# Attention products with V issued two steps at a time, one step's exponentials in the gates' buffers, gates loaded in the last unit

## The chip, the cores and the metric
The kernel runs on one core of a Trainium2 chip. Its engines are TensorE (PE, with its weight loads as PEld), VectorE (DVE), ScalarE (ACT), GpSimd (POOL) and SyncE (SP), which here issues all DMAs, in order. The metric is the device time of one execution in microseconds; lower is better.

## What is computed
Two layers of a backbone that mixes three branches over 1024 latent and 256 context tokens, model width 1024. Each layer normalises and modulates its input, projects it once, and feeds (A) a chunked, bidirectional gated delta recurrence with four heads, (B) attention with four heads, in which latent tokens read latents and context and context tokens read context alone, and (C) a gated short convolution. The outputs are gated, concatenated, sent through one output projection and added to the stream, times a gate; after the last layer only the latents are kept, with a final norm. The core of the attention and of the recurrence in the reference:

```python
def block(q_blk):                                  # attention, per block of 128 queries
    s = jnp.einsum("bqhd,bkhd->bhqk", q_blk, k).astype(F32) * scale
    p = jax.nn.softmax(s, axis=-1).astype(v.dtype)
    return jnp.einsum("bhqk,bkhd->bqhd", p, v)

def step(s, xs):                                   # recurrence, per chunk of 64 tokens
    w_n, u_n, qk_n, qd_n, kd_n, gt_n = xs
    v_new = u_n - jnp.einsum("bhck,bhkv->bhcv", w_n, s)
    o_n = jnp.einsum("bhck,bhkv->bhcv", qd_n, s) + jnp.einsum("bhij,bhjv->bhiv", qk_n, v_new)
    s = s * gt_n[..., None, None] + jnp.einsum("bhck,bhcv->bhkv", kd_n, v_new)
    return s, o_n
...
x = x + gate_x * (mix_x @ w_out)                   # after each layer, and ctx with gate_c in the first
```

## The kernel before
Scores are kept transposed: keys lie on the partitions, queries along the row. The attention of a layer is cut into units of one pair of heads and one group of queries: 512 queries against ten tiles of 128 keys (four units in each layer), and in the first layer two units more of 256 context queries against the two context tiles. A unit of ten key tiles has five steps of two tiles.

A step goes as follows. `a_scores` (L1131) makes, for two key tiles and two heads, four score banks of three products each (a split of the operands in a high and a low part, `kh`, `kl`, or `kc` for the context keys; the products are recorded at line L84) and has ScalarE write their exponentials into two `probT` tiles (L1143). POOL adds the exponentials of all steps up in `vt` (L1129); of the last step, VectorE does one head's part, in a layer's last unit both (L1127). `a_pv` (L1148) issues four products with V (L1159). These are column-tiled: the two heads of the pair write partitions 0 to 63 and 64 to 127 of one bank `po` with a `tile_position` (0, 64r), while the score products fill the whole array. `a_out` (L1162) follows the last step of a unit: two column-tiled products with ones that sum `vt` over the keys (L1170), a reciprocal (L1173), two multiplications (L1174 and, on POOL, L1175) and the store of `bx_d`.

PE's order in this part is the order of the program, written out by hand: the PVs of a step stand behind the scores of the next one, so that ScalarE has a step's time for its exponentials. Between scores, `filler` issues the row maxima of the next unit (`a_max`, L1102, reduced by DVE at L1104), and `sch.tick` moves a planned clock on; lanes whose time has come then issue their next piece. The lanes are the two directions of the recurrence (P products L1226, `vd` and `ring` from DVE L1228 and POOL L1232; V products L1236, DVE L1240, ACT L1244; D products L1249, L1254, L1255; operands arrive in slots of `ring` over SP: vr_d, nn_d, kt_d, qk_d, row_d), the loads of the output weights (`load_wo`, L1311), and the first finish lanes of the output stage (loads of `ot`, `raw`, `za`, `xt`; L1344 to L1354; then the products of `mix` with w_out, recorded at L84). Outside this part a planner orders PE by modelled times, as it does for the other engines everywhere; so an edit can also move PE's rows far away from it.

Buffers are pools by tag: T5 holds five tiles of 128x1024 values, taken by `probT`; B4 two, taken by the context keys' tiles and then by the two gate vectors, `gate_x` and `gate_c` (each broadcast to 128 partitions, 512 KB; in the last layer the second is the final norm's weight); P2 seven, among them `zb` and `wr`. `load_wo` waits for the recurrence to have read its first state, loads both gates, and then 16 pieces `wr` of w_out, which ScalarE (L75, `wo_hi`) and POOL or DVE (L76, `wo_lo`) split. The gates are first used at L1368, in the output stage.

Of the kernel before, what the change touches and what calls it, by code (L numbers as in the profile page):

```python
# [13 lines left out]
D = 1024  # L14
# [8 lines left out]
GROUPS = ((0, 512), (512, 512), (1024, 256))  # L23
# [5 lines left out]
def kernel(  # L29
# [27 lines left out]
    def st(shape, tag, dtype=F32, name=None):  # L57
        return sb.tile(shape, dtype, tag=tag, name=name or tag, bufs=BUFS[tag])

    def const(shape, name, dtype=F32):  # L60
        return sb.tile(shape, dtype, tag=name, name=name, bufs=1)

    def bank():
        return ps.tile([128, 512], F32, tag="b", name="bank", bufs=8)

    def dram(shape, name):
        return dr.tile(shape, F32, tag=name, name=name, bufs=1)

    V, A, P, T, S = nc.vector, nc.scalar, nc.gpsimd, nc.tensor, nc.sync
# [11 lines left out]
    def mm3(outp, pairs):  # L81
        n = len(pairs)
        for q, (lh, rh) in enumerate(pairs):
            T.matmul(outp, lhsT=lh, rhs=rh, start=q == 0, stop=q == n - 1)  # L84
# [36 lines left out]
    sch = Sched()  # L121

    class Flags(dict):
# [3 lines left out]
        def ok(self, *keys):  # L127
# [41 lines left out]
    LY = [dict(A2=const([128, 2, KD], f"A2{l}"), B2=const([128, 2, KD], f"B2{l}"), col=const([128, 102], f"col{l}"),  # L169
               gate=dram([2, D], f"gate_d{l}")) for l in range(DEPTH)]  # L170
# [145 lines left out]
    for l in range(DEPTH):  # L316
        last = l == DEPTH - 1
# [115 lines left out]
        def parts(n_tok):  # L433
            return [(g, t0, n, 2 + t0 if g < 2 else 1030) for g, (t0, n) in enumerate(GROUPS) if t0 < n_tok]
# [485 lines left out]
        if l == 0:  # L920
# [16 lines left out]
            for t in (0, 1):  # L937
                for hf in range(2):
                    pms = [bank(), bank()]
                    for k4 in range(2):  # L940
                        for j in range(2):
                            q = 2 * hf + j
# [47 lines left out]
        for q, b in enumerate(z2):  # L990
            g = parts(n_tok_a)[-1][0]
# [90 lines left out]
        def a_keys(g):  # L1082
            return [8, 9] if g == 2 else list(range(NT))

        def key_tile(h, kt):
            if kt < NX:
                return kh[:, h, kt * 128:(kt + 1) * 128], kl[:, h, kt * 128:(kt + 1) * 128]
            return kc[:, 0, h, (kt - NX) * 128:(kt - NX + 1) * 128], kc[:, 1, h, (kt - NX) * 128:(kt - NX + 1) * 128]
# [21 lines left out]
        def a_shift(u):  # L1110
            m = GROUPS[u["g"]][1] // 128
            pn = bank()
            T.transpose(pn[0:2 * m, 0:128], u["nm"][:, 0:2 * m], ident)
            rw = st([8, 128], "h5", F32R, name="rw")
            copy_a(rw[0:2 * m], pn[0:2 * m, 0:128])
            for r, gh in enumerate(heads(u)):
                S.dma_start(out=Q[gh]["qt"][96:97, 0, 0:128 * m].bitcast(F32).rearrange("p (j t) -> p j t", j=m), in_=rw[r * m:(r + 1) * m].bitcast(F32))

        def a_sums(u, kts, pts, rs=(0, 1)):
            n = GROUPS[u["g"]][1]  # L1120
            keys = a_keys(u["g"])
            for r in rs:
                acc = vt[:, 5 + r, 0:n]
                ab_ = [pts[r][:, kk, 0:n] for kk in range(2)]
                for a0, a1 in [(ab_[0], ab_[1])] if kts[0] == keys[0] else [(acc, ab_[0]), (acc, ab_[1])]:
                    if kts[-1] == keys[-1] and (r == 0 or u is units[-1]):
                        V.tensor_tensor(out=acc, in0=a0, in1=a1, op=ALU.add)  # L1127
                    else:
                        P.tensor_tensor(acc, a0, a1, ALU.add)  # L1129

        def a_scores(u, kts, filler):  # L1131
            g, pair = u["g"], u["pair"]
            n = GROUPS[g][1]
            first = kts[0] == a_keys(g)[0]
            pts = [st([128, 2, 512], "T5", name="probT") for _ in range(2)]
            for kk, kt in enumerate(kts):
                for r in range(2):
                    h = 2 * pair + r
                    qt = Q[g, h]["qt"]
                    hi, lo = key_tile(h, kt)  # L1140
                    pb = bank()[:, 0:n]
                    mm3(pb, [(hi[0:97], qt[0:97, 0, 0:n]), (hi[0:96], qt[0:96, 1, 0:n]), (lo[0:96], qt[0:96, 0, 0:n])])
                    A.activation(out=pts[r][:, kk, 0:n], in_=pb, func=ACTF.Exp)  # L1143
                    if kk and not first:
                        a_sums(u, kts, pts, (r,))
                    sch.tick(0.0014 * n)
                    filler()
            return pts  # L1148

        def a_pv(u, kts, pts):  # L1150
            g, pair = u["g"], u["pair"]
            n = GROUPS[g][1]
            keys = a_keys(g)
            if "po" not in u:
                u["po"] = bank()
            for kk, kt in enumerate(kts):
                for r in range(2):
                    hh = 2 * pair + r
                    T.matmul(u["po"][64 * r:64 * r + 64, 0:n], lhsT=vx[:, kt, hh * 64:hh * 64 + 64], rhs=pts[r][:, kk, 0:n],  # L1159
                             start=kt == keys[0], stop=kt == keys[-1], tile_position=(0, 64 * r))  # L1160
# [121 lines left out]
        def heads(u):  # L1282
            return [(u["g"], 2 * u["pair"] + r) for r in range(2)]
# [21 lines left out]
        nu = len(units)  # L1305
        wo = []

        gates = []
        wof = Flags()

        def load_wo():  # L1311
            while not recurred.ok(0, 1):
                yield 1.0
            for nm, src in (("gate_x", LY[l]["gate"][0]), ("gate_c", final_norm_g if last else LY[l]["gate"][1])):
                gates.append(st([128, D], "B4", name=nm))
                S.dma_start(out=gates[-1], in_=src.partition_broadcast(128))
            for q in range(2):
                wh = st([128, KD, 512], "B16", F32R, name="wo_hi")
                wl = st([128, KD, 512], "B16", F32R, name="wo_lo")
                yield from load_wo_half(q, wh, wl)  # L1320
                wo.append((wh, wl))
            wof.put(0, 3.0)

        def load_wo_half(q, wh, wl):
            for k in range(KD):
                wr = st([128, 512], "P2", name="wr")
                S.dma_start(out=wr, in_=w_out[l, 128 * k:128 * k + 128, 512 * q:512 * q + 512])
                yield 1.5
                split(wr, wh[:, k], wl[:, k], P if k % 2 else V)
                yield 1.5  # L1330
# [70 lines left out]
            hdone.put(i, 1.0)  # L1401

        sch.add(load_wo())
        prev = ending = None
        aheads = []
        for x_, u in enumerate(units):
            keys = a_keys(u["g"])
            steps = [keys[q:q + 2] for q in range(0, len(keys), 2)]
            nxt = units[x_ + 1] if x_ + 1 < nu else None
            if nxt:  # L1410
                mg = a_max(nxt)

            def filler():
                if nxt and (len(steps) == 1 or 1 <= q <= 3):
                    for _ in range(6 if len(steps) == 1 else 2):
                        if next(mg, u) is not u:
                            sch.tick(0.25)

            for q, kts in enumerate(steps):
                if nxt and q == 0:  # L1420
                    sch.until(lambda: nxt["g"] in QA)
                    for gh in heads(nxt):
                        q_head(*gh)
                    sch.tick(2.4)
                    if nxt["pair"] == 1 and nxt["g"] + 1 in qgs:
                        sch.add(q_rows(nxt["g"] + 1))
                if nxt and q == 4:
                    a_shift(nxt)
                pts = a_scores(u, kts, filler)
                if prev:  # L1430
                    a_pv(*prev)
                    if prev[0] is not u:
                        next(ending)
                        for gh in heads(prev[0]):
                            Q.pop(gh)
                    sch.tick(0.0035 * GROUPS[prev[0]["g"]][1])
                if q == 0:
                    a_sums(u, kts, pts)
                if q == len(steps) - 1:
                    ending = a_out(u)  # L1440
                    next(ending)
                prev = (u, kts, pts)
                if nxt and len(steps) == 1:
                    for _ in mg:
                        pass
                    a_shift(nxt)
                if (x_, q) in (((nu - 1, 1), (nu - 1, 3)) if last else ((nu - 3, 3), (nu - 2, 0))):
                    sch.until(lambda: len(recurred) == 2)
                    ahead(len(aheads))
                    aheads.append(q)  # L1450
        a_pv(*prev)
        Q.clear()
        ahead(2)
        sch.tick(2.0)
# [94 lines left out]
```

## Time and profile before
| | us |
|---|---|
| median of three runs | 1718.66 (1716.41 to 1720.2) |
| the profiled execution, its own time | 1723.55 |
| its span on the core | 1721.8 |
| PE busy | 1650.5 (96%) |
| PE at L1159, products with V | 79.4 |
| ACT at L1143, exponentials | 96.5 |
| POOL at L1129, sums | 144.7 |

Attention of layer 0 takes about 590 to 818 us of the span, that of layer 1 about 1420 to 1632. A row of a timeline is a group of like instructions that follow one another: its start, the time from the first start to the last end, the line and the shapes, the count of records, and in brackets the idle time before it with what ended it. Ends of matmuls are modelled, so the distance from a group's start to the next group's start is the better measure of what it took.

### The profile page before, as it was taken

How to read it: one execution, taken by the hardware profiler on the slowest of the kernel's cores; microseconds unless marked ns; L12 is line 12 of the kernel's file. 1: busy time of each engine (PE TensorE's matmuls, PEld its weight loads, DVE VectorE, ACT ScalarE, POOL GpSimd, SP SyncE). 2: the span in 40 equal slices, each digit the busy share in tenths (PEclk: the TensorE clock that was granted, in tenths of full speed). 3: DMA queues.
4: the chain of work that ended last, by engine and by line, in shares of the span. 5: the costliest groups of instructions: out<-in, count | busy, mean ns of one | idle time of the engine just before them, and what ended most of it. 6: DMA issues, size and time to landing. Idle time of an engine off the chain costs nothing.

```text
span 1721.8 us, 29896 instructions
## 1 busy us (share of the span) xinstructions
PE 1650.5 (96%) x10964; PEld 1316.9 (76%) x10964; DVE 1101.9 (64%) x2041; ACT 758.8 (44%) x1909; POOL 646.3 (38%) x848
## 2 busy tenths in 40 slices
PE   7999999999999999998999999999999989999998
PEld 5887888787887877764888887787778778776586
DVE  2534668878643767765565346689797377776664
ACT  4644565223444534344354435652245444434432
POOL 0520345321320456557331212544232136556731
PEclk8999999999999899999999999999999989999999
DMA  9332464753254755544443314556524465454551
GB/s 360 124 126 79 155 196 150 242 178 123 78 160 125 257 157 177 186 144 159 132 141 111 104 56 134 161 179 224 166 70 128 151 211 164 160 188 156 172 159 49
DMA packets 195403, 266.54 MB, mean 155 GB/s; under 512 B 50529, under 2 KB 115249, under 8 KB 195257
## 3 DMA queue, kind: packets, MB, share of 16 engines
q1 hardware_dynamic: 195256, 264.64, 47.8%
q8 instruction: 87, 1.43, 0.3%
q14 instruction: 60, 0.48, 0.1%
HBM read 182.71 MB, written 79.17 MB: 152 GB/s over the span
## 4 chain that ended last, share of the span: by engine, by line
PE 68%; DVE 10%; DMA 9%; issue 5%; ACT 3%; POOL 3%; SPq 1%; POOLq 0%; DVEq 0%; ACTq 0%
PE bank L452 26%; PE bank L84 22%; PE bank L1159 3%; PE bank L1236 2%; PE bank L1255 2%; PE bank L1249 2%; DVE pr L680 2%; PE bank L1254 2%; PE bank L1102 2%; DMA gcb<-row_d 2%; DVE Mb L681 1%; DMA wa<-in_w_ada_dram 1%; PE bank L1226 1%; DVE acc L466 1%; PE bank L516 1%
## 5 line engine op out<-in xcount | busy, mean ns | idle before, releaser
L452 PE MATMUL bank<-h_hi,w 128*128 128x512 f32 x1664 | 432.5, 403 | 2.4 <-DVE h_hi L283 2.4
L452 PEld LDWEIGHTS bank<-h_hi,w 128*128 128x128 f32 x1664 | 305.4, 190 | 74.6 <-issue 4.5
L452 PE MATMUL bank<-h_lo,w 128*128 128x512 f32 x832 | 217.7, 402 | 0.0
L452 PEld LDWEIGHTS bank<-h_lo,w 128*128 128x128 f32 x832 | 154.3, 189 | 37.0 <-issue 1.6
L466 DVE SCALAR_TENSOR_TENSOR acc<-pad,col,acc 128x1284 f32<-128x1284 f32 (+1 forms) x104 | 160.1, 1540 | 11.1 <-ACT acc L463 9.5
L1129 POOL TENSOR_TENSOR vt<-vt,probT 128x512 f32<-128x512 f32 x110 | 144.7, 1335 | 20.2 <-ACT probT L1143 19.5
L84 PE MATMUL bank<-wo_hi,mix 128*128 128x512 f32 x576 | 145.0, 402 | 1.8 <-ACT wo_hi L75 1.1
L1143 ACT ACTIVATE probT<-bank 128x512 f32<-128x512 f32 (+1 forms) x168 | 96.5, 590 | 98.2 <-PE bank L84 92.2
L84 PEld LDWEIGHTS bank<-wo_hi,mix 128*128 128x128 f32 x576 | 108.2, 191 | 28.6 <-ACT wo_hi L75 2.6
L76 DVE TENSOR_TENSOR w<-wr,w 128x1024 fp32r<-128x1024 f32 x52 | 66.6, 1283 | 93.3 <-ACT w L75 93.3
L1104 DVE TENSOR_REDUCE mx<-bank 128x1 f32<-128x512 f32 (+1 forms) x200 | 108.5, 585 | 10.9 <-PE bank L1102 9.7
L452 PE MATMUL bank<-h_c,w 128*128 128x256 f32 x816 | 109.7, 287 | 0.0
L452 PEld LDWEIGHTS bank<-h_c,w 128*128 128x128 f32 x816 | 102.2, 190 | 5.8 <-issue 3.7
L75 ACT ACTIVATE w<-wr 128x1024 fp32r<-128x1024 f32 x52 | 54.9, 1060 | 75.3 <-PE bank L452 56.3
L84 PE MATMUL bank<-qt,kh 97*128 97x512 f32 (+1 forms) x256 | 84.4, 411 | 3.5 <-ACT probT L1143 2.8
L1159 PE MATMUL bank<-probT,vt 128*64 128x512 f32 (+1 forms) x336 | 79.4, 594 | 0.0
L1232 POOL TENSOR_TENSOR ring<-ring,qx 128x512 f32<-128x512 f32 x32 | 40.9, 1277 | 92.7 <-DMA ring<-row_d 76.8
L680 DVE TENSOR_TENSOR pr<-L,Mb 128x31 f32<-128x31 f32 (+15 forms) x186 | 70.7, 380 | 4.6
L84 PE MATMUL bank<-wo_lo,mix 128*128 128x512 f32 x288 | 73.5, 395 | 0.0
L681 DVE TENSOR_TENSOR Mb<-Mb,pr 128x31 f32<-128x31 f32 (+15 forms) x186 | 68.6, 369 | 5.0
L617 POOL TENSOR_TENSOR gcb<-gcb,gc 128x1024 f32<-128x1024 f32 x20 | 44.5, 2231 | 62.7 <-DMA gcb<-row_d 36.8
L79 ACT ACTIVATE pad<-bank 128x512 f32<-128x512 f32 (+1 forms) x78 | 41.0, 531 | 54.1 <-PE bank L452 39.1
(310 smaller groups left out, 3225.2 us busy)
## 6 DMA issues: line engine op xcount, KB each, us to landing
wr<-in_w_blk_dram SPq DMA_DIRECT2D x52, 512.0 KB
wa<-in_w_ada_dram SPq DMA_DIRECT2D x32, 512.0 KB
gcb<-row_d SPq DMA_DIRECT2D x20, 512.0 KB
nn_d<-N SPq DMA_DIRECT2D x20, 512.0 KB
ring<-vr_d SPq DMA_DIRECT2D x40, 256.0 KB
ring<-nn_d SPq DMA_DIRECT2D x40, 256.0 KB
qk_d<-gcb SPq DMA_DIRECT2D x18, 512.0 KB
ring<-kt_d SPq DMA_DIRECT2D x36, 256.0 KB
```

Source lines behind the costliest of these rows:

```text
L75: A.activation(out=hi, in_=raw, func=ACTF.Copy)
L76: eng.tensor_tensor(out=lo, in0=raw, in1=hi.bitcast(F32), op=ALU.subtract)
L84: T.matmul(outp, lhsT=lh, rhs=rh, start=q == 0, stop=q == n - 1)
L452: T.matmul(pb[:, 0:n], lhsT=self.w[:, wi, k, :], rhs=hg[g][hi][:, k, :], start=q + k == 0, stop=q == 2 and k == KD - 1)
L466: V.scalar_tensor_tensor(out=acc[:, 2:hi], in0=pad[:, 2 + t - r:hi + t - r], scalar=col[:, ci:ci + 1], in1=acc[:, 2:hi], op0=ALU.mult, op1 ...
L617: P.tensor_tensor(gcb, gcb, bc(gc[:, i, :], 128), ALU.subtract)
L680: V.tensor_tensor(out=pv, in0=bc(L[:, 0:k, k], w), in1=N[:, k:k + 1, k:32].to_broadcast([128, k, w]), op=ALU.mult)
L681: V.tensor_tensor(out=N[:, 0:k, k:32], in0=N[:, 0:k, k:32], in1=pv, op=ALU.subtract)
L1104: V.tensor_reduce(mx[:, gk:gk + 1], pb[:, 0:n], AX.X, ALU.max)
L1129: P.tensor_tensor(acc, a0, a1, ALU.add)
L1143: A.activation(out=pts[r][:, kk, 0:n], in_=pb, func=ACTF.Exp)
L1159: T.matmul(u["po"][64 * r:64 * r + 64, 0:n], lhsT=vx[:, kt, hh * 64:hh * 64 + 64], rhs=pts[r][:, kk, 0:n], start=kt == keys[0], stop=kt == ...
```

## The change
The order of `a_pv` changes. A list `prev` collects steps. At even steps (0, 2, 4) all that it holds are issued, each followed by its tick: at step 0 the last step of the unit before, at step 2 the PVs of steps 0 and 1, at step 4 those of steps 2 and 3. The exponentials of the step that starts at key tile 4 (step 2) go into B4 instead of T5. The gates are loaded by a function of its own in the last unit, at step 2 (or in a unit of one step), and not at the start of `load_wo`; since a `probT` tile of a step 2 holds each B4 buffer then, a load waits for that tile's PVs and sums.

```diff
-            pts = [st([128, 2, 512], "T5", name="probT") for _ in range(2)]
+            pts = [st([128, 2, 512], "B4" if kts[0] == 4 else "T5", name="probT") for _ in range(2)]
...
         def load_wo():
             while not recurred.ok(0, 1):
                 yield 1.0
-            for nm, src in (("gate_x", LY[l]["gate"][0]), ("gate_c", final_norm_g if last else LY[l]["gate"][1])):
-                gates.append(st([128, D], "B4", name=nm))
-                S.dma_start(out=gates[-1], in_=src.partition_broadcast(128))
...
+        def load_gates():
+            for nm, src in (("gate_x", LY[l]["gate"][0]), ("gate_c", final_norm_g if last else LY[l]["gate"][1])):
+                gates.append(st([128, D], "B4", name=nm))
+                S.dma_start(out=gates[-1], in_=src.partition_broadcast(128))
...
-        prev = ending = None
+        prev, ending = [], None
...
-                if prev:
-                    a_pv(*prev)
-                    if prev[0] is not u:
+                if q % 2 == 0:
+                    for st_ in prev:
+                        a_pv(*st_)
+                        sch.tick(0.0035 * GROUPS[st_[0]["g"]][1])
+                    if prev and prev[0][0] is not u:
                         next(ending)
-                        for gh in heads(prev[0]):
+                        for gh in heads(prev[0][0]):
                             Q.pop(gh)
-                    sch.tick(0.0035 * GROUPS[prev[0]["g"]][1])
+                    prev.clear()
+                    st_ = None
...
-                prev = (u, kts, pts)
+                prev.append((u, kts, pts))
+                pts = None
+                if x_ == nu - 1 and (q == 2 or len(steps) == 1):
+                    load_gates()
...
-        a_pv(*prev)
+        a_pv(*prev.pop())
```

PE, the end of layer 1's last unit, before. L1159 are PVs, `kc` the scores of the context keys, L1353 products of a finish lane, L1170 the sums' products.

```order
L1159 MATMUL bank<-probT,vt 64x512 x4
L84 MATMUL bank<-qt,kc 128x512 x12
L1159 MATMUL bank<-probT,vt 64x512 x8
L1353 MATMUL bank<-cst,ot_15718 128x128 x4
L1170 MATMUL bank<-vt,cst 64x512
L1353 MATMUL bank<-cst,ot_15804 128x128 x4
L84 MATMUL bank<-wo_hi,mix 128x512 x7
L1170 MATMUL bank<-vt,cst 64x512
L84 MATMUL bank<-wo_hi,mix 128x512 x9
L84 MATMUL bank<-wo_lo,mix 128x512 x8
```

The same place after:

```order
L84 MATMUL bank<-qt,kc 128x512 x12
L1159 MATMUL bank<-probT,vt 64x512 x12
L1355 MATMUL bank<-cst,ot_15711 128x128 x4
L1170 MATMUL bank<-vt,cst 64x512
L1355 MATMUL bank<-cst,ot_15802 128x128 x4
L1170 MATMUL bank<-vt,cst 64x512
L84 MATMUL bank<-wo_hi,mix 128x512 x16
L84 MATMUL bank<-wo_lo,mix 128x512 x8
```

The PVs of step 2, which stood apart, are in one run with those of steps 3 and 4; both sums' products stand ahead of all products with `wo_hi`, which are sixteen in a row.

PE, layer 1, the end of its second unit, before: L1226 and L1236 are P and V products of the recurrence, L1113 a transposition, `qa` and `qb` the next queries.

```order
L1159 MATMUL bank<-probT,vt 64x512 x4
L1226 MATMUL bank<-ring_13693,kx 128x128 x8
L1113 MATMUL bank<-cst,nm 8x128
L84 MATMUL bank<-qt,kc 128x512 x12
L1159 MATMUL bank<-probT,vt 64x512 x4
L1236 MATMUL bank<-ring_13692 128x128 x4
L1236 MATMUL bank<-ring_13693 128x128 x4
L84 MATMUL bank<-qa,wq 128x512 x3
```

The same place after:

```order
L1113 MATMUL bank<-cst,nm 8x128
L84 MATMUL bank<-qt,kc 128x512 x3
L1226 MATMUL bank<-ring_13693,kx 128x128 x8
L84 MATMUL bank<-qt,kc 128x512 x9
L1159 MATMUL bank<-probT,vt 64x512 x4
L1236 MATMUL bank<-ring_13692 128x128 x4
L1236 MATMUL bank<-ring_13693 128x128 x4
L1159 MATMUL bank<-probT,vt 64x512 x4
L84 MATMUL bank<-qa,wq 128x512 x3
```

The PVs of steps 2 and 3 should follow one another here, and the tick between them lets the V products L1236 in; in each layer two pairs are parted in this way.

PE, layer 1's projection, far from the attention, before: L452 are full-array products of the projection, L746 and L755 products of 64x64 that prepare the recurrence, L516 transpositions.

```order
L452 MATMUL bank<-h_hi,w 128x512 x4
L452 MATMUL bank<-h_c,w 128x256 x16
L755 MATMUL bank<-N,tt 64x64 x8
L746 MATMUL bank<-tt,Mm 64x64 x8
L452 MATMUL bank<-h_c,w 128x256 x8
L452 MATMUL bank<-h_hi,w 128x512 x8
L452 MATMUL bank<-h_lo,w 128x512 x8
L452 MATMUL bank<-h_hi,w 128x512 x5
L755 MATMUL bank<-N,tt 64x64 x8
L452 MATMUL bank<-h_hi,w 128x512 x3
```

The same place after:

```order
L452 MATMUL bank<-h_hi,w 128x512 x2
L452 MATMUL bank<-h_c,w 128x256 x16
L755 MATMUL bank<-N,tt 64x64 x8
L452 MATMUL bank<-h_c,w 128x256 x8
L746 MATMUL bank<-tt,Mm 64x64
L452 MATMUL bank<-h_hi,w 128x512 x5
L746 MATMUL bank<-tt,Mm 64x64 x7
L452 MATMUL bank<-h_hi,w 128x512 x3
L452 MATMUL bank<-h_lo,w 128x512 x8
L452 MATMUL bank<-h_hi,w 128x512 x8
L755 MATMUL bank<-N,tt 64x64 x8
```

L746, which followed L755 without a product between, stands apart from it, in two pieces.

SP, layer 1's third unit, before: row_d, vr_d and qk_d are operands of the recurrence's last stage, bx_d is the store of `a_out`.

```order
L1269 DMA o_d<-ot 128x512
L1201 DMA ring_13692<-nn_d 128x512
L1265 DMA ot<-o_d 128x512 x4
L1176 DMA bx_d<-zb 128x512
L1204 DMA ring_13692<-qk_d 128x512
L1327 DMA wr<-in_w_out_dram 128x512 x2
L1201 DMA ring_13692<-vr_d 128x512
L1207 DMA ring_13692<-row_d 128x512
```

The same place after:

```order
L1269 DMA o_d<-ot 128x512
L1201 DMA ring_13692<-nn_d 128x512
L1265 DMA ot<-o_d 128x512 x4
L1204 DMA ring_13692<-qk_d 128x512
L1329 DMA wr<-in_w_out_dram 128x512
L1201 DMA ring_13692<-vr_d 128x512
L1207 DMA ring_13692<-row_d 128x512
L1329 DMA wr<-in_w_out_dram 128x512
L1176 DMA bx_d<-zb 128x512
```

The store bx_d stood ahead of the last qk_d, vr_d and row_d, and now stands behind them.

## Rows read from the trace of the kernel before
**Rows 1.** Page, part 1: busy us of each engine, share of the span, instructions.
```profile
PE 1650.5 (96%) x10964; PEld 1316.9 (76%) x10964; DVE 1101.9 (64%) x2041; ACT 758.8 (44%) x1909; POOL 646.3 (38%) x848
```

**Rows 2.** PE's waits, 590 to 820 us: us in total, times, longest.
```profile
PE bank L84 <- ACT probT L1143: 2.2, 2, 1.9
...
PE bank L1102 <- ACT ring L1244: 1.1, 1, 1.1
```

**Rows 3.** PE's waits, 1420 to 1632 us.
```profile
PE bank L1170 <- DVE vt L1127: 3.1, 1, 3.1
PE bank L1236 <- ACT probT L1143: 1.4, 1, 1.4
PE bank L1102 <- DVE ring L1228: 1.2, 1, 1.2
```

**Rows 4.** PE's timeline, layer 1's last unit: start, us, instruction, count, [idle before].
```profile
1594.48 0.62 PE L84 MATMUL bank<-qt,kh 97*128 97x512 f32 x2
1594.94 0.40 PE L84 MATMUL bank<-qt,kl 96*128 96x512 f32 x1
1595.27 1.94 PE L1159 MATMUL bank<-probT,vt 128*64 128x512 f32 x8
1597.13 0.74 PE L84 MATMUL bank<-qt,kh 97*128 97x512 f32 x2
1597.71 0.39 PE L84 MATMUL bank<-qt,kl 96*128 96x512 f32 x1
...
1610.41 3.65 PE L1159 MATMUL bank<-probT,vt 128*64 128x512 f32 x16
1614.00 0.66 PE L1353 MATMUL bank<-cst,ot 128*128 128x128 f32 x4
1617.76 1.97 PE L1170 MATMUL bank<-vt,cst 128*64 128x512 f32 x2 [3.10 <-DVE vt L1127]
```

**Rows 5.** PE's timeline, layer 1's projection, 1240 to 1250 us.
```profile
1240.26 0.86 PE L452 MATMUL bank<-h_hi,w 128*128 128x512 f32 x3
1241.05 0.68 PE L746 MATMUL bank<-tt,Mm 64*64 64x64 f32 x16
...
1243.63 2.13 PE L452 MATMUL bank<-h_hi,w 128*128 128x512 f32 x8
1245.61 2.03 PE L452 MATMUL bank<-h_lo,w 128*128 128x512 f32 x8
1247.47 3.90 PE L452 MATMUL bank<-h_hi,w 128*128 128x512 f32 x16
```

**Rows 6.** ACT's timeline, layer 1, the recurrence's last stage.
```profile
1566.90 1.15 ACT L75 ACTIVATE wo_hi<-wr 128x512 fp32r<-128x512 f32 x2 [5.38 <-POOL ring L1232]
```

**Rows 7.** POOL's timeline, layer 1, last stage and last unit.
```profile
1565.60 1.27 POOL L1232 TENSOR_TENSOR ring<-ring,qx 128x512 f32<-128x512 f32 x1 [8.85 <-DMA ring<-row_d]
...
1592.63 3.00 POOL L1129 TENSOR_TENSOR vt<-probT 128x512 f32<-128x512 f32 x2
...
1606.77 9.12 POOL L1129 TENSOR_TENSOR vt<-vt,probT 128x512 f32<-128x512 f32 x7
```

**Rows 8.** SP's timeline: the gates' loads, and the stretch ahead of row_d.
```profile
577.78 0.32 SPq L1316 DMA_DIRECT2D gate_x<-gate_d  x1
...
1404.28 0.33 SPq L1316 DMA_DIRECT2D gate_c<-in_final_norm_g_dram  x1
...
1555.55 0.32 SPq L1176 DMA_DIRECT2D bx_d<-zb  x1
...
1558.58 0.42 SPq L1207 DMA_DIRECT2D ring<-row_d  x1
```

**Rows 9.** Windows: busy us of each engine (instructions), PEclk, DMA share, GB/s.
```profile
785.00:790.00 5.00, 5.00 (x25) 2.69 (x21) 1.92 (x2) 2.65 (x5) 4.92 (x5) 1.00 0.04 11
...
1615.00:1620.00 5.00, 2.24 (x4) 0.63 (x5) 5.00 (x6) 1.78 (x3) 2.53 (x2) 0.74 0.75 268
1620.00:1625.00 5.00, 5.00 (x20) 3.33 (x19) 2.84 (x3) 1.28 (x3) 1.74 (x2) 0.92 0.97 346
```

**Rows 10.** Page, part 5: exponentials; busy, mean ns | idle before, releaser.
```profile
L1143 ACT ACTIVATE probT<-bank 128x512 f32<-128x512 f32 (+1 forms) x168 | 96.5, 590 | 98.2 <-PE bank L84 92.2
```

## Prediction
> **What bounds the kernel now.** The first view to read is the page's list of busy times: TensorE (PE) works for 96% of the span, VectorE, ScalarE and GpSimd (POOL) for less than two thirds of it [rows 1]. So nearly every microsecond is PE's, and a change gains where it makes PE's own work shorter or ends one of its waits. The second view is what PE waited for in the two attention stretches. In layer 0 the waits that a change of order could touch sum to about 3.3 us [rows 2], in layer 1 to 5.7 us [rows 3], of which 3.1 us stand in front of one instruction, the sums' product L1170 at the very end. The third view is PE's timeline there, since the change touches no amount of work, only how often PE goes from full-array products to the column-tiled ones (128x64) and back.
>
> **The price of one switch.** In the last unit of layer 1, two 512-wide score products start 0.46 us apart as a pair (1594.48 to 1594.94), so one takes 0.23 us. The last one ahead of a group of four PVs (the trace books two records for each product, so x8) takes from 1594.94 to 1595.27, which is 0.33: 0.10 more. The group takes 1.86 to the next start (1595.27 to 1597.13). The double group takes 3.59 (1610.41 to 1614.00): a second four adds 1.73, so 0.13 of each run is paid once. The first pair of full-array products behind it takes 0.58 (1597.13 to 1597.71) against 0.46: 0.12 more. A column-tiled run thus costs 0.10 + 0.13 + 0.12 = 0.35 us beside its work [rows 4]. [...]
>
> **What the change does to PE's order.** Counting runs of PV and L1170 rows without other products between them, before has 43 and after 33, five fewer in each layer. Sixteen pairs of steps are issued together, but the tick between the two PVs lets a recurrence lane in: in each layer two pairs are split by the V products of L1236, as the second place in the order shows, and some sums' products lose a PV neighbour. Term one: 10 x 0.35 = **-3.5 us**.
>
> The planner's times also shift elsewhere. In layer 1's projection, a 64x64 run that was one (L755 with L746 behind it) comes apart, and one L746 group is cut into one and seven: two runs more. Their price: the three products ahead of L746 take 0.79 (1240.26 to 1241.05), against 3 x 0.2325 from eight undisturbed ones that take 1.86 (1245.61 to 1247.47): 0.09 more. The eight behind L755 take 1.98 (1243.63 to 1245.61), 0.12 more than 1.86. That is 0.21 with nothing for the inside of the run, and 0.35 if it drains as the other does [rows 5]. I take the upper end, since the switch is of the same kind. Term two: 2 x 0.35 = **+0.7 us** (bounds +0.4 and +0.7).
>
> **What of it counts.** Everywhere but in layer 1's last unit PE ends last, so the runs removed are time removed. There, POOL does: its adds of L1129 run without a gap, "9.12 us x7" at the end [rows 7], and PE idles 3.10 us for the sum [rows 4]. That unit loses two of the ten runs (four to two). Reaching the wait 0.7 us earlier only lengthens it. Term three: **+0.7 us**. The second sums' product, which stood behind seven w_out products, now stands ahead of them, as the first place in the order shows; I cost that at nothing, since the w_out products behind it need tiles that come out of the same queues.
>
> **Gates.** Removing two 512 KB loads at the start of attention (577.78 in layer 0) and at 1404.28 in layer 1 [rows 8] frees queue time nobody waited for: I cost it at nothing; no PE wait of rows 2 and 3 is of that time. They come back in the last unit, where each must wait for a step-2 tile of B4 to be read by its PVs and by POOL's adds. SP issues in order, so behind them stand, in layer 0, raw, wr and a zb load, and in layer 1 four xt and eight wr loads with the second half of w_out. In layer 0 the DMA share in 785 to 790 us is 0.04, so they land in an idle time; cost nothing. In layer 1 the share is 0.75 and then 0.97 at 346 GB/s up to 1625 us [rows 9]: 1 MB more there takes at most 1,048,576 B / 346 GB/s = 3.0 us, if nothing hides it. Bounds 0 and +3.0; I take 0, since in the row behind PE is busy all five us while the DMAs are full, and ScalarE, which splits w_out, has had slack throughout [rows 9, 10].
>
> **Buffers and the recurrence.** With step 2's exponentials in B4, T5 carries four of five steps, so a PV that comes a step later meets no shortage: the tile that step q+1 takes is the one of a pair already consumed. Cost nothing; if that cover failed, ScalarE would wait for a PV group, 1.86 us. The recurrence loses PV work that lay between its P (L1226) and V (L1236) products in some stages and gets it back in others; bounds -2 and +2 us in each layer, from the stalls of rows 2 and 3, taken at 0 since in the changed order the shortest such stretch, with the durations of these rows, is still some 3.3 us of PE work.
>
> **Sum.** -3.5 + 0.7 + 0.7 = **-2.1 us**. Against the profiled execution (span 1721.8, 1723.55 with what lies around it) that is 1721.45; this execution is 4.89 above the median of the runs, 1718.66, and on that scale the forecast is **1716.6 us**, its own range 1714.3 to 1718.7.
>
> **Rival A: the stalls of the last recurrence stages go too.** ScalarE stood 5.38 us ahead of wo_hi (1566.90), since POOL's last L1232 needed a row_d load [rows 6, 7]. SP issued that load at 1558.58, behind a bx_d store that it issued at 1555.55 once POOL's zb was ready [rows 8]. After, row_d is ahead of bx_d in both layers. For it: PE's waits behind this chain are 2.2 + 1.1 us and 1.4 + 1.2 [rows 2, 3], together 5.9. Against it: the load needs a ring slot that PE frees only shortly before, and PE comes to its V products earlier too. If two thirds go: -2.1 - 4.0, **1712.6 us**.
>
> **Rival B, the slower side: bursts of eight scores.** Before, four PVs (1.86 us [rows 4]) stand behind every four scores, and cover ScalarE when it is late; after, every second step has none. A score takes PE three products, 0.70 us, and an exponential takes ScalarE 0.59 [rows 10]: a burst gains ScalarE only 8 x 0.11 = 0.9 us for its other work. Each time that ScalarE's queue stands still in a step without PVs (as 5.38 us before wo_hi [rows 6]), PE may wait up to 1.86 us more. The places are the waits on probT and on ring, some five of them [rows 2, 3]. Two such places (3.7 us) eat the gain, three make the kernel measurably slower; four give -2.1 + 7.4, **1724.0 us**. Against it: over all exponentials ScalarE waited 92.2 us for PE [rows 10], and PE for probT less than 4. By the Trainium skill, TensorEngine Tiling (Array Packing), section PSUM Bottleneck, column tiling speeds up TensorE but not the evacuation of PSUM, which is this rival: in front of a longer tiled stretch comes a longer stretch that only ScalarE empties. The row on exponentials speaks against it, the waits at the recurrence for it.
>
> **Rival C: it does not come to time.** The saved runs are swallowed by waits on the recurrence and on POOL, as in the last unit, and the gates cost a part of their 3.0 us [rows 9]: **1718.7 us**.
>
> **How the numbers follow.** Forecast 0.47, A 0.21, B 0.18, C 0.14. What a measurement of this kernel tells from no change is about 0.2%, 3.4 us: under 1715.2 is faster, over 1722.1 slower. Of the forecast's cases a quarter lie under 1715.2 (0.12), nearly all of A (0.21): faster 0.33. Of B most lie over 1722.1 (0.16), with C's worst (0.01): slower 0.17. Same: the rest, 0.50. The range leaves out the upper half of B and the lower third of A: 1711.8 to 1722.8.
>
> **What would show it.** In the profile after: PV rows of x16 in most units, followed by one slow pair of scores (0.58) and not two; a last unit whose L1170 starts at the same distance from the first L1129 add of that unit, some 25 us [rows 4, 7], with a longer PE wait ahead of it; PE's waits on probT and ring of the same size as in rows 2 and 3 (smaller by some 4 us together: A; larger by 2 us in each of several: B). The gates are right if no wo_hi wait grows. I would be wrong if a double run of eight PVs took twice 1.86, or if the waits on probT became the largest of the stretch.

## The result: slower by 0.9%

| | before | after |
|---|---|---|
| median, us | 1718.59 (6 runs) | 1734.59 (6 runs) |
| lowest to highest, us | 1715.5 to 1722.85 | 1731.43 to 1736.28 |
| ratio, 95% interval | | 1.009 [1.0071, 1.0108] |
| profiled execution: its time, span | 1723.55, 1721.8 | 1736.08, 1734.3 |

The forecast was 1716.6 us, with 1722.8 as its upper end. The changed kernel has ten runs of column-tiled products less, as counted, and is 16 us slower. One execution of before, of 3193.82 us, was in the slow state, and the 1718.63 us that stands beside e15, e16 and e17 below is the median without it. The page of after, to hold against [rows 1]:

```profile
PE 1652.9 (95%) x10964; PEld 1320.5 (76%) x10964; DVE 1107.7 (64%) x2041; ACT 760.0 (44%) x1909; POOL 643.1 (37%) x848
```

PE's idle time is 1734.3 - 1652.9 = 81.4 us, against 71.3 before. What PE waited for in the whole span of after (us in total, times, longest):

```profile
PE bank L1113 <- DVE nm L1107: 12.7, 8, 2.1
...
PE bank L1170 <- DVE vt L1127: 4.1, 1, 4.1
...
PE bank L84 <- DMA qtc<-rw: 3.2, 1, 3.2
PE bank L84 <- ACT probT L1143: 2.8, 2, 2.0
PE bank L84 <- ACT wo_hi L75: 2.6, 3, 1.6
...
PE bank L1102 <- ACT probT L1143: 2.2, 4, 0.8
```

The first line is the one that matters. L1113 is the transposition of a unit's row maxima, in `a_shift`; the same line of before reads

```profile
PE bank L1113 <- DVE nm L1107: 4.3, 2, 2.1
```

Two waits of 2.1 us, one ahead of each layer's first unit, are in both kernels. Six waits, three in each layer, are new, and sum to 8.4 us. The first of them, in before and then in after, on PE's timeline (start, us, instruction, count, [idle before]):

```profile
632.99 0.28 PE L1102 MATMUL bank<-kc,qt 96*128 96x256 f32 x1
633.20 1.94 PE L1159 MATMUL bank<-probT,vt 128*64 128x512 f32 x8
635.07 2.05 PE L1226 MATMUL bank<-ring,kx 128*128 128x128 f32 x16
636.96 0.27 PE L1113 MATMUL bank<-cst,nm 128*8 128x128 f32 x1
```

```profile
629.12 0.28 PE L1102 MATMUL bank<-kc,qt 96*128 96x256 f32 x1
630.58 0.27 PE L1113 MATMUL bank<-cst,nm 128*8 128x128 f32 x1 [1.19 <-DVE nm L1107]
630.61 0.95 PE L84 MATMUL bank<-qt,kc 97*128 97x512 f32 x3
```

And VectorE at the same two places:

```profile
633.19 1.02 DVE L1104 TENSOR_REDUCE mx<-bank 128x1 f32<-128x512 f32 x2
634.24 0.16 DVE L1107 TENSOR_REDUCE nm<-mx 128x1 f32<-128x3 f32 x1
```

```profile
629.32 1.02 DVE L1104 TENSOR_REDUCE mx<-bank 128x1 f32<-128x512 f32 x2
630.37 0.16 DVE L1107 TENSOR_REDUCE nm<-mx 128x1 f32<-128x3 f32 x1
```

From the last product with keys (L1102) VectorE needs some 1.4 us until `nm` is there, in both kernels. Before, PE had the PVs of step 2 and a recurrence stage to do meanwhile, 3.8 us; after, the PVs of step 2 stand a step later, the ticks of lanes went with them, and L1113 is next.

### The profile page after: what moved, and what is told of

It reads as the page before. It is cut to its first block, busy times and chain, and to the rows that moved or that the text cites. A ratio compares the mean times of both kernels' runs of the same rounds, so it can differ in the third digit from the quotient of the medians.

```text
span 1734.3 us, 29881 instructions
## 1 busy us (share of the span) xinstructions
PE 1652.9 (95%) x10964; PEld 1320.5 (76%) x10964; DVE 1107.7 (64%) x2041; ACT 760.0 (44%) x1909; POOL 643.1 (37%) x848
## 4 chain that ended last, share of the span: by engine, by line
PE 71%; DVE 12%; DMA 7%; issue 4%; ACT 3%; POOL 2%; SPq 1%; DVEq 0%; POOLq 0%; ACTq 0%
PE bank L452 27%; PE bank L84 22%; PE bank L1159 4%; PE bank L1236 2%; DVE pr L680 2%; PE bank L1255 2%; PE bank L1249 2%; PE bank L1254 2%; DVE Mb L681 2%; PE bank L1102 1%; DVE mx L1104 1%; DVE acc L466 1%; PE bank L1226 1%; DMA wa<-in_w_ada_dram 1%; PE bank L516 1%
## 5 line engine op out<-in xcount | busy, mean ns | idle before, releaser
L452 PE MATMUL bank<-h_hi,w 128*128 128x512 f32 x1664 | 432.9, 403 | 2.4 <-DVE h_hi L283 2.4
L452 PEld LDWEIGHTS bank<-h_hi,w 128*128 128x128 f32 x1664 | 305.3, 190 | 74.8 <-issue 4.5
L452 PE MATMUL bank<-h_lo,w 128*128 128x512 f32 x832 | 216.2, 400 | 0.0
L452 PEld LDWEIGHTS bank<-h_lo,w 128*128 128x128 f32 x832 | 153.2, 188 | 36.7 <-issue 1.6
L84 PE MATMUL bank<-wo_hi,mix 128*128 128x512 f32 x576 | 145.2, 403 | 2.9 <-ACT wo_hi L75 2.6
L84 PEld LDWEIGHTS bank<-wo_hi,mix 128*128 128x128 f32 x576 | 108.6, 191 | 30.8 <-ACT wo_hi L75 3.7
L452 PE MATMUL bank<-h_c,w 128*128 128x256 f32 x816 | 110.5, 289 | 0.0
L452 PEld LDWEIGHTS bank<-h_c,w 128*128 128x128 f32 x816 | 103.1, 191 | 5.8 <-issue 3.7
L84 PE MATMUL bank<-qt,kh 97*128 97x512 f32 (+1 forms) x256 | 84.4, 411 | 3.0 <-ACT probT L1143 2.8
L1159 PE MATMUL bank<-probT,vt 128*64 128x512 f32 (+1 forms) x336 | 77.8, 598 | 0.0
L84 PE MATMUL bank<-wo_lo,mix 128*128 128x512 f32 x288 | 73.3, 395 | 0.0
```

The costliest lines, as they stand in the source:

```text
L452: T.matmul(pb[:, 0:n], lhsT=self.w[:, wi, k, :], rhs=hg[g][hi][:, k, :], start=q + k == 0, stop=q == 2 and k == KD - 1)
```

## Where the 12.5 us of the two traces lie

Stretches of PE's timeline between the same instructions, in us, from each kernel's trace:

| stretch | before | after | after, second trace |
|---|---|---|---|
| start to layer 0's first L1113 | 582.71 | 581.20 | 580.35 |
| to the first product of mix with wo_hi (layer 0's attention) | 224.40 | 231.40 | 233.17 |
| to the next layer's first L188 (output stage) | 201.57 | 202.93 | 202.71 |
| to layer 1's first L1102 (projection) | 374.60 | 375.48 | 376.41 |
| to layer 1's first L1113 | 28.71 | 28.44 | 28.14 |
| to the end (layer 1's attention and output) | 309.81 | 314.85 | 314.92 |

The second and the last row carry 7.0 + 5.0 = 12.0 of the 12.5 us. Their sum is called attention below, though it includes layer 1's output stage; from the first L1113 to the last PVs alone, the two layers take 421.4 us before, 432.4 after and 434.3 in the second trace. The six new waits are 8.4 of the 12.0. At two places the clock falls behind them, which costs 1.4 us more each time, as shown next; the rest is not divided here. Before has only one trace, of an execution 5 us above its median, so differences of a microsecond or two against it are not to be read closely. PE's timeline of after at the second place in layer 0:

```profile
692.28 0.28 PE L1102 MATMUL bank<-kc,qt 96*128 96x256 f32 x1
694.34 0.27 PE L1113 MATMUL bank<-cst,nm 128*8 128x128 f32 x1 [1.79 <-DVE nm L1107]
694.37 2.76 PE L84 MATMUL bank<-qt,kc 97*128 97x512 f32 x9
696.93 1.91 PE L1236 MATMUL bank<-ring,ring 128*128 128x128 f32 x8
698.63 1.48 PE L1236 MATMUL bank<-ring 128*128 128x128 f32 x8
...
700.74 3.65 PE L1159 MATMUL bank<-probT,vt 128*64 128x512 f32 x16
704.33 1.16 PE L1249 MATMUL bank<-vd,ring 128*128 128x128 f32 x8
```

and the same stretch in windows (busy us of each engine with instructions, granted clock, DMA share, GB/s):

```profile
692.00:694.00 2.00, 0.55 (x3) 0.20 (x2) 2.00 (x6) 0.60 (x1) 1.60 (x2) 1.00 0.85 310
694.00:696.00 2.00, 1.66 (x8) 1.40 (x9) 0.25 (x2) 0.85 (x2) 1.40 (x2) 1.00 0.05 17
696.00:698.00 2.00, 2.00 (x10) 1.76 (x9) 1.78 (x2) 1.21 (x3) 1.92 (x2) 0.52 0.01 2
698.00:700.00 2.00, 2.00 (x13) 2.00 (x13) 1.97 (x2) 0.00 (x1) 0.81 (x1) 0.62 0.13 22
700.00:702.00 2.00, 2.00 (x10) 0.82 (x11) 0.69 (x1) 2.00 (x8) 0.23 (x1) 1.00 0.74 213
```

The granted clock falls to 0.52 and 0.62, which is the lower of its two levels (1.2 against 2.4 GHz) for most of four microseconds. The four products of 696.93 (two records each) take 1.70 us to the next start; in e2_shift_later, where the clock holds, the same four take 0.89 (below). From L1113 to the PVs at 700.74 PE has twelve score products and eight of L1236 to do, which take 4.94 us there (690.86 to 696.72, less a wait of 0.92) and 6.37 here: 1.4 us lost behind a wait of 1.79. The fall comes again at the sister place of layer 1, where the same products take 6.36 us, and in the second trace of the same kernel at both (6.36 each). The windows of before at these two places, and then that of after in layer 1:

```profile
695.00:700.00 5.00, 5.00 (x33) 4.18 (x33) 3.47 (x9) 2.09 (x5) 3.02 (x3) 1.00 0.56 211
...
1530.00:1535.00 5.00, 5.00 (x37) 4.61 (x37) 3.31 (x5) 3.19 (x9) 1.27 (x1) 1.00 0.58 175
```

```profile
1530.00:1535.00 5.00, 4.44 (x19) 3.96 (x20) 2.09 (x4) 2.06 (x4) 3.29 (x3) 0.74 0.00 1
```

## Experiments

The forecast had no theory that holds, so three were set against each other. **T**: the PVs of step 2 covered VectorE's last row maxima, and L1113 waits for them now. **B**: bursts of eight scores without PVs starve PE of exponentials (the forecast's rival B). **G**: the late gates.

**e1_cover_gone.** The kernel before, with only the cover taken away.

```diff
-                if nxt and q == 4:
-                    a_shift(nxt)
                 pts = a_scores(u, kts, filler)
+                if nxt and q == 3:
+                    a_shift(nxt)
                 if prev:
                     a_pv(*prev)
```

> The kernel before with one thing taken from it: the transposition of the row maxima (L1113) is issued behind the scores of step 3 and ahead of that step's group of four PVs, where it stood behind them; runs of PVs, buffers and gates stay. Theory T (the changed kernel is slower because L1113 lost the PV group that covered the last row maxima on VectorE): PE's waits of L1113 for nm rise from 4.3 us to about 12.7, and the clock falls once behind the longest of them in each layer, so +9 to +14 us against the kernel before, some 1730 us. Theory B (bursts of eight scores starve ScalarE): no change beyond 1 us, since bursts stay at four. Theory G (late gates): no change.

Measured: 1726.8 against 1720.86 us, 1.0037 [1.0021, 1.0053]. PE's waits, whole span:

```profile
PE bank L1113 <- DVE nm L1107: 13.0, 8, 2.2
```

The waits are all there with no burst and no late gate; B and G expected no change. Behind the longest of the new waits in each layer the clock falls, as T said: to 0.66 in 755 to 760 us, behind a wait of 1.64, and to 0.75 in 1580 to 1585 us, behind one of 1.59. The time rose by 6 us, less than T's 9. By stretches its attention is longer by 6.05 and 3.7 us, 9.7 in sum (8.8 up to the last PVs), as T has it; but layer 0's output stage is shorter by 4.6 us (196.95 against 201.57), with another order of PE's products there. That stage comes in two lengths in these programs, 201.6 to 202.9 us (before, after, e4, e15, e16) and 196.6 to 198.3 (e1, e2, e7, e10, e13, e14), with e9 between them at 199.9, and an edit in the attention can tip it. Among the longer ones, before and e4 have one order of PE's products in that stage, and after, e15 and e16 another. Any two programs should be compared by stretches for that reason.

**e2_shift_later.** The changed kernel, with L1113 behind the first two scores of step 4 (called by `filler`, which runs after each score).

```diff
-                if nxt and q == 4:
-                    a_shift(nxt)
+                late = 2 if nxt and q == 4 else 0
...
             def filler():
+                nonlocal late
+                if late:
+                    late -= 1
+                    if not late:
+                        a_shift(nxt)
```

> The changed kernel with the transposition of the row maxima issued behind the first two scores of step 4 and not ahead of them: two scores, 1.4 us of PE work, stand between the last row maxima and L1113. Theory T: L1113's waits fall from 12.7 us to under 6 (the two of 2.1 ahead of the first units stay), the clock no longer falls there, so -8 to -11 us against the changed kernel, some 1724 us. Theories B and G: still about 1734.

Measured: 1720.86 us, less than T gave, ratio to before 1.0 [0.9986, 1.0015]; some 14 us less than the changed kernel. PE at the place shown above, and its waits at L1113:

```profile
690.86 1.55 PE L84 MATMUL bank<-qt,kc 97*128 97x512 f32 x6
693.32 0.27 PE L1113 MATMUL bank<-cst,nm 128*8 128x128 f32 x1 [0.92 <-DVE nm L1107]
693.35 0.95 PE L84 MATMUL bank<-qt,kc 97*128 97x512 f32 x3
694.14 1.06 PE L1236 MATMUL bank<-ring,ring 128*128 128x128 f32 x8
695.03 1.06 PE L1236 MATMUL bank<-ring 128*128 128x128 f32 x8
695.84 0.95 PE L84 MATMUL bank<-qt,kc 97*128 97x512 f32 x3
```

```profile
PE bank L1113 <- DVE nm L1107: 6.2, 4, 2.2
```

Waits fell by 6.5 us, the clock stays at 1.00 in 695 to 700 us, and the bursts and the late gates are still in: B and G are out as main causes. Attention is 536.8 us, 9.5 less than in the changed kernel; 4.6 more came from layer 0's output stage, which T has nothing to say of.

**e16_pair23, e15_pair01 and e17_after_again.** The change by halves, and itself, on one chip. `if q % 2 == 0` becomes `if q != 3` (only steps 2 and 3 together) or `if q != 1` (only steps 0 and 1).

> The changed kernel with only the PVs of steps 2 and 3 issued together; those of steps 0 and 1 stand alone. 41 runs of PVs and sums. Theory T: L1113 has lost its cover in six units as in the changed kernel (12.7 us of waits), so nearly all of its loss stays, 1730 us or more. Theory B: half of the loss, 1726 us.

> The changed kernel with only the PVs of steps 0 and 1 issued together; those of step 2 stand behind the scores of step 3 again, ahead of L1113. 39 runs of PVs and sums. Theory T: L1113's waits are back at 4.3 us, no fall of the clock there, so four runs by 0.35 us less than the kernel before, within 2 us of it (1718 to 1721 us). Theory B (a burst of eight scores is enough): half of the changed kernel's loss stays, 1726 or more.

> The changed kernel itself, beside the two halves and on their chip, with a second trace. L1113's waits again 12.7 us; what is asked of the trace is whether the falls of the clock behind them (690 to 700 and 1530 to 1540 us) and in the output stage of layer 0 (820 to 830 us) come again. Time 1732 to 1737 us.

Measured against 1718.63 us: pair 2 and 3 1732.02, 1.0086 [1.0054, 1.0118]; pair 0 and 1 1722.23, 1.0024 [1.0003, 1.0044]; the changed kernel 1733.79, 1.0087 [1.0049, 1.0126]. L1113 in e16 and then in e15:

```profile
PE bank L1113 <- DVE nm L1107: 12.7, 8, 2.2
```

```profile
PE bank L1113 <- DVE nm L1107: 4.3, 2, 2.2
```

One of the two pairs carries most of the loss, 13.4 of 15.2 us, the one whose PVs stood ahead of L1113. The other costs more than it saves, and its time lies just above the 1718 to 1721 that T gave: four runs fewer should have given 1.4 us, and the kernel is 3.6 slower. In its trace attention is 1.9 us longer than before. Up to the last PVs it is 0.6 shorter; the loss stands behind them, where L1170 waits 5.8 us in layer 1 (3.1 before), and no experiment here says why.

**e4_gates_late.** The kernel before with `load_gates` of the change, and nothing else.

> The kernel before with only the loads of the gates moved to the last unit, as in the changed kernel; PVs and buffers of exponentials stay. Theory G: the wait for qtc grows by 1 us and the clock falls there, and w_out comes late in layer 1: +3 to +7 us. Theory T: within 2 us of the kernel before.

Measured: 1719.76 us, 0.9994 [0.9983, 1.0005]. The gates cost nothing, and the wait for qtc, which is 3.2 us in the changed kernel, is 2.0 here as in before, so the gates are not what lengthened it:

```profile
PE bank L84 <- DMA qtc<-rw: 2.0, 1, 2.0
```

**e7_pairs_odd.** Pairs moved by one step, so that eight PVs precede L1113.

```diff
-            pts = [st([128, 2, 512], "B4" if kts[0] == 4 else "T5", name="probT") for _ in range(2)]
+            pts = [st([128, 2, 512], "B4" if kts[0] == 6 else "T5", name="probT") for _ in range(2)]
...
-                if q % 2 == 0:
+                if q in (0, 1, 3):
...
-        a_pv(*prev.pop())
+        for st_ in prev:
+            a_pv(*st_)
...
-                if x_ == nu - 1 and (q == 2 or len(steps) == 1):
+                if x_ == nu - 1 and (q == 3 or len(steps) == 1):
```

> The changed kernel with the pairs moved by one step: the PVs of steps 1 and 2 are issued at step 3 and those of steps 3 and 4 at step 0 of the next unit, step 0's alone at step 1; step 3's exponentials are those in the gates' buffers, and the gates are loaded at step 3 of the last unit. Eight PVs stand between the row maxima and L1113 in every unit, and the runs of PVs and sums are 35 (33 in the changed kernel, 43 before). Theory T: L1113's waits are back at 4.3 us, and eight runs saved are -2.8 us, so some 1715 to 1718 us. Theory B: bursts of eight scores remain, so still 1728 or more. Theory G: still 1728 or more.

Measured: 1726.28 us, 1.0029 [1.0015, 1.0042]: the expectation of T was missed. L1113's waits are back at 4.3 us, but PE's timeline ahead of layer 1's last unit reads

```profile
1578.37 3.65 PE L1159 MATMUL bank<-probT,vt 128*64 128x512 f32 x16
1581.95 0.27 PE L1113 MATMUL bank<-cst,nm 128*8 128x128 f32 x1
1581.98 3.05 PE L84 MATMUL bank<-qt,kc 97*128 97x512 f32 x12
1586.80 1.22 PE L84 MATMUL bank<-qt,kh 97*128 97x512 f32 x2 [1.77 <-DMA qt<-rw]
```

The pair takes 3.6 us, more cover than VectorE needs, and only step 4's scores stand between L1113 and the next unit, which waits for the transposed row to come back through a DMA; the pair of 1586.80 then takes 1.02 us instead of 0.58, at a granted clock of 0.67 in 1585 to 1590 us. From this L1113 to the last PVs it is 32.6 us, against 28.7 before. L1113 has two neighbours: too little ahead of it, and it waits; too little behind, and its result is late. Another wait, 4.08 us for wo_hi, is new in the output stage, and was not followed up.

**e13_maxima_earlier, e14_earlier_no_tick, e10_before_maxima and e9_no_tick.** The cover given back in another way: the row maxima end two scores earlier (first line). In e14 the two PVs of a pair also keep together (the rest), which e9 does to e2_shift_later; e10 puts the first line alone into the kernel before, as a control.

```diff
-                    for _ in range(6 if len(steps) == 1 else 2):
+                    for _ in range(6 if len(steps) == 1 else 3 if q == 2 else 2):
...
                     for st_ in prev:
                         a_pv(*st_)
+                    for st_ in prev:
                         sch.tick(0.0035 * GROUPS[st_[0]["g"]][1])
```

> The changed kernel with the row maxima issued at three pieces for each score of step 2 (two in steps 1 and 3, as before), so that the last one stands two scores ahead of L1113, which stays where it is. Theory T (L1113's lost cover is the cause, whichever way it is given back): its six waits of 1.2 to 1.8 us vanish or fall under 0.5, the clock does not fall there, and the time is that of e2_shift_later or less, 1717 to 1721 us. If instead it was the later place of L1113 that helped in e2_shift_later (by a shift of the lanes, or of what waits on the transposed rows), the time stays above 1728 us.

> e13_maxima_earlier with both ticks of a pair behind its second PV group: 30 runs of PVs and sums (36 in e13_maxima_earlier). Six runs by 0.35 us: 2 us less than e13_maxima_earlier, so 1715 to 1719 us, if the recurrence does not answer.

> The kernel before with the row maxima issued as in e13_maxima_earlier, the control for it: PVs stay single (43 runs or so), the gates early. L1113 did not wait there before, so no change: within 2 us of the kernel before. The difference of e13_maxima_earlier from this one is then the worth of pairing itself, by the forecast's step -0.35 us for each run saved, some -2 us.

> The kernel of e2_shift_later with both ticks of a pair behind its second PV group, so that no lane comes between them: 30 runs of PVs and sums (34 in e2_shift_later, 43 before). If a run saved is worth 0.35 us wherever PE ends last, -1.4 us against e2_shift_later, some 1719.5; if the recurrence, which steps two ticks later, answers with waits, 1722 or more.

Measured, against 1720.01 us:

| | runs of PVs and sums | median, us | ratio to before | attention, us (before 534.2, after 546.3) |
|---|---|---|---|---|
| e10_before_maxima | 44 | 1721.94 | 1.0012 [0.9999, 1.0024] | 540.4 |
| e13_maxima_earlier | 36 | 1721.07 | 1.0006 [0.9991, 1.002] | 538.7 |
| e14_earlier_no_tick | 30 | 1717.69 | 0.998 [0.9969, 0.9992] | 536.2 |
| e9_no_tick | 30 | 1719.33 | 0.9999 [0.9985, 1.0014] | 535.5 |

e13 gives back the changed kernel's loss with L1113 at its old place, so it is the wait and not the place. Its waits at L1113:

```profile
PE bank L1113 <- DVE nm L1107: 5.2, 4, 2.2
```

Between e10, e13 and e14, which have the same maxima, the time falls as the runs do: e14 has 14 runs fewer than e10 and 4.25 us less, 0.30 us for each (0.35 in the forecast), and in attention alone 4.1. The steps are uneven, though: 0.9 us for the eight runs between e10 and e13, less than expected and within the intervals, and 3.4 us for the six between e13 and e14. Also, PE waits 8.8 us for exponentials in e10's trace and 7.1 in e14's, so the 0.30 us agree with the forecast's price but do not measure it alone. Pairing can pay when nothing is uncovered by it. PE in e14 at both places:

```profile
631.93 0.27 PE L1113 MATMUL bank<-cst,nm 128*8 128x128 f32 x1
631.96 3.04 PE L84 MATMUL bank<-qt,kc 97*128 97x512 f32 x12
634.92 3.65 PE L1159 MATMUL bank<-probT,vt 128*64 128x512 f32 x16
...
691.84 0.27 PE L1113 MATMUL bank<-cst,nm 128*8 128x128 f32 x1 [0.46 <-DVE nm L1107]
```

e14 beats both kernels, by 0.2% the one before and by some 1% the changed one. What it has over the kernel before does not lie in attention, though, which is 2 us longer there than before: it is in the shorter of the two output stages (197.4 us) and in the projection (372.8 against 374.6). Moving the maxima may have a price of its own (e10's trace: a wait of 5.0 us for exponentials in layer 0), though e10's time cannot be told from before's. In e9 the ticks alone bring nothing that can be told from e2_shift_later, 1719.33 against 1720.86 us with the runs of before at 1720.01 and 1720.86; its waits at L1113 are back at 1.8 and 2.2 us in one unit of each layer.

## Why the prediction was wrong

- **The step that failed** is the one on what the PVs covered. The text asked of the moved PVs whether their buffers and the recurrence's stretches could do without them, and took both at 0; it named no other consumer. The PVs of step 2 were also the work behind which VectorE finished the last row maxima for L1113. The first unit's stretch in before shows it with two rows (L1113 without idle time at 636.96, `nm` ready at 634.40), and the forecast's own second place in the order has L1113 behind a PV group and a P stage in before and without either in after. No row of an idle engine points there: a wait that is covered leaves none. Six times 1.2 to 1.8 us, 8.4 us, were left out. Nor did the forecast's two signs of being wrong look there: a double run does not take twice 1.86 us, and the waits on probT are not the largest.
- **The clock** had no term. Behind the two waits of 1.79 us it fell to its lower level, at 1.4 us a time. The forecast priced waits at their length. The falls near 740 and 800 us in the changed kernel are another matter: e2, e10 and e14 have them too, and the single trace of before does not, so that trace flatters before there. Over the whole span the mean granted clock is 0.978 in both kernels' profiled executions.
- **The price of a switch** was right where rows show it: all eleven double groups of after take 3.58 to 3.64 us, as the one in [rows 4] did (3.59), and single groups between full-array products still take 1.86 or 1.87. e14 against e10 gives 0.30 us for a run, which agrees. The count of ten runs was right. "The runs removed are time removed" was not, since other waits moved up.
- **Rival B** had the right shape, a PV group gone from where it covered another engine, and 1.86 us for each place as the upper end, but the wrong engine and place: it looked at ScalarE's exponentials (PE's waits for probT went from 2.8 us at L84 and 1.4 at L1236 to 2.8 at L84 and 2.2 at L1102, 0.8 more in all) and missed VectorE's maxima.
- **Rival A** did not come in layer 0: the stall of its last stage is there, 2.0 us for probT, and row_d ahead of bx_d did not end it. In layer 1 the two stalls of [rows 3] at L1236 and L1102, 2.6 us, are gone, with 0.8 and 0.4 us on probT in their place; what ended them was not tested.
- **Gates and layer 1's last unit** were right: e4 shows no cost of the gates, and L1170's wait grew from 3.10 to 4.06 us, which agrees with the forecast's 0.7 us of saving that turns into waiting. The two 64x64 runs cannot be told: the projection is 0.9 us longer in after, but e2 to e16 scatter by more.
- The growth of the wait for qtc from 2.0 to 3.2 us stays open; it is in e2, e7 and e14 too (3.2 to 3.3) and not in e4, so it comes with the pairs, not with the gates.

## What to carry to other kernels

Before work is moved away from a place on the busiest engine, list every instruction that stands behind it there, with what each needs and when that is ready; a wait that the work covers has no idle row and shows only as the distance from the producer's end to the consumer's start. Saving switches is worth its small price only where that list is empty, or is emptied first, by issuing the producer earlier. And compare two programs stretch by stretch, since an edit at one place can tip a stage elsewhere by more than it saves.

## What was not expected of the hardware

A wait of 1.79 us is followed by a fall to the lower level, 1.2 GHz, after PE had been busy again for some 2 us, in both traces of the changed kernel and at both sister places; waits of 0.92 and 1.03 us at the same places (e2) are not. It is not the length of the wait alone: in e9 waits of 1.84 and 2.16 us stand at these places without a fall, while in e1 it falls behind 1.64 and 1.59 us in the third units and not behind 1.55 us here. In before a wait of 1.87 us [rows 2] stood without a fall in 740 to 745 us (1.00), and in after a wait of 2.02 us there came with 0.55. What decides it stays open. Where the clock fell in a busy stretch of the output stage, it cost as much as the wait right ahead of it. PE in after (granted clock 0.58 in 825 to 830 us), and in e2_shift_later (1.00 in 820 to 825 us):

```profile
825.07 1.09 PE L1355 MATMUL bank<-cst,ot 128*128 128x128 f32 x4 [1.51 <-DVE ot L1351]
825.81 5.52 PE L84 MATMUL bank<-wo_hi,mix 128*128 128x512 f32 x16
831.18 0.39 PE L84 MATMUL bank<-wo_lo,mix 128*128 128x512 f32 x1
```

```profile
818.41 3.98 PE L84 MATMUL bank<-wo_hi,mix 128*128 128x512 f32 x16
822.23 0.63 PE L84 MATMUL bank<-wo_lo,mix 128*128 128x512 f32 x2
```

Sixteen products take 5.37 us in after and 3.82 in e2, 1.55 more, behind a wait of 1.51 us. In e2 one wait of 2.41 us stands ahead of them, in after four that sum to 4.1 within 8 us.
